# Attention of a hybrid decoder: scores and products that alternate between the two heads of a pair

## Chip, cores and metric

The kernel runs on one core of a Trainium2 chip. The metric is the device time of one execution in microseconds; a profile of one execution shows what each engine did. PE is TensorE (PEld its weight loads), DVE is VectorE, ACT is ScalarE, SP issues the DMAs.

## What is computed

Two decoder layers on 256 tokens of width 1024, everything in float32. Each layer projects the normalised tokens once and gives the columns to three mixers (a convolution, NSA attention and dilated attention), joins them with an output projection, and adds a feed-forward block with a short convolution. Cut to what bears on the change:

```python
for l in range(2):
    h = rms_norm(x, attn_norm[l])
    parts = split(h @ w_in[l])
    y_a = conv_module(...)          # 31 taps
    y_b = nsa_mixer(...)            # 8 query heads of 64, 2 key heads; compressed + selected + window
    y_c = dilated_mixer(...)        # 4 heads, 3 groups (widths 128/512/2048, strides 1/4/16)
    x = x + concat(y_a, y_b, y_c) @ w_out[l]
    x = x + conv_ffn(rms_norm(x, ffn_norm[l]), ...)

def masked_softmax(s, mask):        # in every attention
    s = where(mask, s, -1e30)
    e = where(mask, exp(s - max(s)), 0)
    return e / sum(e)
```

## The kernel before

Tokens are two tiles of 128. The dense projections split each f32 operand into a high and a low part and make three matmuls of them (L412 to L414); the weights arrive by DMA in pieces of 128 x 1024 or so, ScalarE writes the high part (L209), VectorE the low part (L212). The dense matmuls of the dilated queries, keys and values (tiles Dq, Dk, Dv) and of the output projection (oa, ob) stand around the attention work on PE.

Heads come in pairs: head j of a pair has its 64 features in partitions 64j to 64j+63 of the query and key tiles, and its output in partitions 64j to 64j+63 of the output bank. A score matmul of one head therefore reads half of the partitions (its shape is shown as 64*128), and a product matmul writes half of them (128*64). All are plain f32, and each shows as two records in the trace.

`nsa_pair(pair)`: for the first 128 queries one matmul per head (L699) fills one half of the score tile `sc` each; four masked minima (L703) read it. The scores are stored with the opposite sign, so the minimum stands for the maximum. For the second 128 queries (L710, L711) each head takes the tile in turn: its scores against 256 keys of the first kind in one bank, against 16 compressed and 256 window keys in the other, then two masked minima (L714) and one addition for the compressed keys. Then ScalarE takes exponentials and scales (L721, L725, L209), PE transposes the probabilities (L737, L743), and ScalarE copies them to `pT`. `nsa_finish(g)` multiplies them with the values: per head four matmuls (L775, L776), then one for the compressed part (L777), all into the one output bank `o`.

`dil_scores(jp)`: for the first 128 queries three matmuls per head (L847), one masked minimum each (L850); for the second, three matmuls of 256 keys per head (L857) and one masked minimum over 768 columns (L859), head by head, each followed by its exponentials (L863), transposes (L869, L876) and copies to `dpT`. `dil_pv(jp)`: six matmuls per head (L888, L890).

The score tile `sc` covers two banks of PSUM and there is one of it, so whoever writes it next waits until it has been read. Steps are written down in this order in each layer:

```python
ORDER = "np(0) dq(0) t(6) np(1) dk(0) t(6) nf(0) np(2) dv(0) t(6) np(3) nf(1) da(0) dq(1) t(10) dk(1) t(100) ds(1) dv(1) ct(0) pv(1)"
```

(np = `nsa_pair`, nf = `nsa_finish`, dq/dk/dv = dilated projections, t = convolution taps on VectorE, ds/pv = `dil_scores`/`dil_pv`, da both, ct = end of the convolution.) The framework's planner turns this into a fixed order for each engine when the program is built: it takes the earliest step whose inputs it believes ready by its own costs, and fills with later ones. So matmuls of Dq stand between the scores of np(0) in the trace. On the chip each engine works through its fixed order and waits where an input is late.

Of the kernel before, what the change touches and what calls it, by code (L numbers as in the profile page):

```python
# [12 lines left out]
F32 = mybir.dt.float32  # L13
# [3 lines left out]
ALU = mybir.AluOpType  # L17
AX = mybir.AxisListType

P = 128  # L20
D = 1024
KT = D // P
S = 256
# [164 lines left out]
def tile_hybrid_trunk(ctx, tc, x_in, pos_in, stream, feats, gains, norms, const_in, out):  # L188
# [13 lines left out]
    def sc_bank(nm):  # L202
        return ps.tile([P, 1024], F32, tag="sc", name=nm, bufs=1)
# [260 lines left out]
    for l in range(L):  # L464
# [222 lines left out]
        def nsa_pair(pair):  # L687
                g, pr = divmod(pair, 2)
                if pr == 0:
                    nsa_state[g] = (mp.tile([P, NT, 4, 16], F32, tag="cs", name=f"cs{g}", bufs=2), [])  # L690
                cs, pTs = nsa_state[g]
                negm = mp.tile([P, 2, 2, 2], F32, tag="negm", name=f"negm{pair}", bufs=2)
                dd = mp.tile([P, 2, 2, 2], F32, tag="dd", name=f"dd{pair}", bufs=2)
                ms0 = mp.tile([P, 2, 2, P], F32, tag="ms", name=f"ms0{pair}", bufs=4)
                msl = [mp.tile([P, 2, 2, P], F32, tag="ms", name=f"ms1{pair}{j}", bufs=4) for j in range(2)]
                sc = sc_bank(f"sc0{pair}")
                for j in range(2):
                    hp_ = slice(j * 64, j * 64 + 64)
                    nc.tensor.matmul(sc[:, j * 512:j * 512 + 272], QT[hp_, pair, 0:P], KG[g][hp_, P:P + 272], start=True, stop=True)  # L699
                for j in range(2):  # L700
                    for w in range(2):
                        o = j * 512 + w * 144
                        nc.vector.tensor_tensor_reduce(out=ms0[:, j, w, :], in0=sc[:, o:o + P], in1=edge[:, P:2 * P], op0=ALU.add, op1=ALU.min,  # L703
                                                       scale=1.0, scalar=3.0e38, accum_out=negm[:, 0, j, w:w + 1])
                tt(cs[:, 0, 2 * pr:2 * pr + 2, :], sc.rearrange("p (j c) -> p j c", j=2)[:, :, P:P + 16],
                   cmadd[:, 0, :].unsqueeze(1).broadcast_to([P, 2, 16]), ALU.add)
                for j in range(2):
                    hp_ = slice(j * 64, j * 64 + 64)
                    sc = sc_bank(f"sc1{pair}{j}")
                    nc.tensor.matmul(sc[:, 0:256], QT[hp_, pair, P:2 * P], KG[g][hp_, 0:256], start=True, stop=True)  # L710
                    nc.tensor.matmul(sc[:, 512:784], QT[hp_, pair, P:2 * P], KG[g][hp_, 256:528], start=True, stop=True)  # L711
                    for w in range(2):
                        o = w * 528
                        nc.vector.tensor_tensor_reduce(out=msl[j][:, w].rearrange("p a b -> p (a b)"), in0=sc[:, o:o + 256],  # L714
                                                       in1=edge[:, P - w * P:3 * P - w * P], op0=ALU.add, op1=ALU.min,
                                                       scale=1.0, scalar=3.0e38, accum_out=negm[:, 1, j, w:w + 1])
                    tt(cs[:, 1, 2 * pr + j, :], sc[:, 512:528], cmadd[:, 1, :], ALU.add)
                for j in range(2):
                    for w in range(2):
                        m = ms0[:, j, w, :]  # L720
                        nc.scalar.activation(out=m, in_=m, func=AF.Exp, scale=-1.0, bias=negm[:, 0, j, w:w + 1], accum_out=dd[:, 0, j, w:w + 1])  # L721
                for j in range(2):
                    for w in range(2):
                        m = msl[j][:, w]
                        nc.scalar.activation(out=m, in_=m, func=AF.Exp, scale=-1.0, bias=negm[:, 1, j, w:w + 1], accum_out=dd[:, 1, j, w:w + 1])  # L725
                ddf = dd.rearrange("p q j w -> p (q j w)")
                nc.vector.reciprocal(out=ddf, in_=ddf)
                gv = sg.rearrange("p t (h s) -> p t h s", s=3)[:, :, 2 * pair:2 * pair + 2, 1:3]
                tt(dd, dd, gv, ALU.mult)
                pT2 = []  # L730
                for j in range(2):
                    pT = mp.tile([P, 3, 3, P], F32, tag="pT", name=f"pT{pair}{j}", bufs=4)[:, 0:2]
                    for w in range(2):
                        copy_act(ms0[:, j, w, :], ms0[:, j, w, :], scale=dd[:, 0, j, w:w + 1])
                    tp = tp_bank(f"tp0{pair}{j}")
                    for w in range(2):
                        nc.tensor.transpose(tp[:, w * P:(w + 1) * P], ms0[:, j, w, :], ident)  # L737
                    copy_act(pT[:, :, 0, :], tp[:, 0:256].rearrange("p (a c) -> p a c", a=2))
                    for w in range(2):
                        copy_act(msl[j][:, w], msl[j][:, w], scale=dd[:, 1, j, w:w + 1])  # L740
                    tp = tp_bank(f"tp1{pair}{j}")
                    for i, (w, e) in enumerate(((0, 1), (0, 0), (1, 0), (1, 1))):
                        nc.tensor.transpose(tp[:, i * P:(i + 1) * P], msl[j][:, w, e, :], ident)  # L743
                    copy_act(pT[:, :, 1:3, :], tp.rearrange("p (a k c) -> p a k c", a=2, k=2))
                    pT2.append(pT)
                pTs.append(pT2)

        def nsa_finish(g):
# [18 lines left out]
            for pr in range(2):  # L767
                pair = 2 * g + pr
                ob = o_bank(f"o{pair}")
                for j in range(2):  # L770
                    pT = pTs[pr][j]
                    os_ = ob[j * 64:j * 64 + 64, 0:S]
                    for w in range(2):
                        vv = [vN[:, t, w, g * 64:g * 64 + 64] for t in range(NT)]
                        nc.tensor.matmul(os_, vv[0], pT[:, w, 0:2, :].rearrange("p a c -> p (a c)"), start=(w == 0), stop=False, skip_group_check=True)  # L775
                        nc.tensor.matmul(os_[:, P:S], vv[1], pT[:, w, 2, :], start=False, stop=False, skip_group_check=True)  # L776
                nc.tensor.matmul(ob[:, 0:S], vbig[:, g, 2 * pr:2 * pr + 2].rearrange("p a d -> p (a d)"), pc, start=False, stop=True, skip_group_check=True)  # L777
                copy_act(yT_hi[:, 2 + pair, :], ob[:, 0:S])
                tt(yT_lo[:, 2 + pair, :], ob[:, 0:S], yT_hi[:, 2 + pair, :].bitcast(F32), ALU.subtract)
# [56 lines left out]
        def dil_scores(jp):  # L836
# [4 lines left out]
            pTs = []  # L841
            m0s = []
            sc = sc_bank(f"dsc0{jp}")
            for j in range(2):
                hp_ = slice(j * 64, j * 64 + 64)
                for g in range(3):
                    nc.tensor.matmul(sc[:, j * 512 + g * P:j * 512 + (g + 1) * P], dq[hp_, g, 0:P], dk[hp_, g, 0:P], start=True, stop=True)  # L847
            for j in range(2):
                m0 = mp.tile([P, 3, P], F32, tag="ms", name=f"dm0{jp}{j}", bufs=4)
                nc.vector.tensor_tensor_reduce(out=m0, in0=sc[:, j * 512:j * 512 + 384].rearrange("p (g c) -> p g c", g=3), in1=dm[:, :, P:2 * P],  # L850
                                               op0=ALU.add, op1=ALU.min, scale=1.0, scalar=3.0e38, accum_out=negm[:, 0, j:j + 1])
                m0s.append(m0)
            for j in range(2):
                hp_ = slice(j * 64, j * 64 + 64)
                sc = sc_bank(f"dsc1{jp}{j}")
                for g in range(3):
                    nc.tensor.matmul(sc[:, g * 256:(g + 1) * 256], dq[hp_, g, P:S], dk[hp_, g, :], start=True, stop=True)  # L857
                m1 = mp.tile([P, 768], F32, tag="ms", name=f"dm1{jp}{j}", bufs=4)
                nc.vector.tensor_tensor_reduce(out=m1, in0=sc[:, 0:768], in1=dilm, op0=ALU.add, op1=ALU.min, scale=1.0, scalar=3.0e38,  # L859
                                               accum_out=negm[:, 1, j:j + 1])  # L860
                m0 = m0s[j].rearrange("p g c -> p (g c)")
                for q, m in ((0, m0), (1, m1)):
                    nc.scalar.activation(out=m, in_=m, func=AF.Exp, scale=-1.0, bias=negm[:, q, j:j + 1], accum_out=dd[:, q, j:j + 1])  # L863
# [17 lines left out]
        def dil_pv(jp):  # L881
            dv, pTs = dil_state["v"], dil_state["p"]
            ob = (tp_bank if jp else o_bank)(f"do{jp}")
            for j in range(2):
                os_ = ob[j * 64:j * 64 + 64, 0:S]
                for g in range(3):
                    c = (2 * g + j) * 64
                    nc.tensor.matmul(os_, dv[:, 0, c:c + 64], pTs[j][:, g, 0:2, :].rearrange("p a c -> p (a c)"), start=(g == 0), stop=False,  # L888
                                     skip_group_check=True)
                    nc.tensor.matmul(os_[:, P:S], dv[:, 1, c:c + 64], pTs[j][:, g, 2, :], start=False, stop=(g == 2), skip_group_check=True)  # L890
            copy_act(yT_hi[:, 6 + jp, :], ob[:, 0:S])
            tt(yT_lo[:, 6 + jp, :], ob[:, 0:S], yT_hi[:, 6 + jp, :].bitcast(F32), ALU.subtract)

# [142 lines left out]
```

## Time and profile before

| | |
|---|---|
| median of 3 runs | 777.91 us (777.12 to 778.69) |
| span of the profiled execution | 776.1 us; the page gives no other time of it |
| busy: PE, VectorE, ScalarE | 751.1, 598.8, 489.9 us |
| attention stretches | 74 to 190 us (layer 0), 453 to 568 us (layer 1) |

The span runs from the first to the last instruction. A matmul's end is modelled, so a group's length is best read from its start to the start of the group that follows. In the views in order of time a row gives start, length, engine, line, operation, the tiles written and read, shape and the number of records merged; rows of one line that overlap others are merged too.

### The profile page before, as it was taken

How to read it: one execution, taken by the hardware profiler on the slowest of the kernel's cores; microseconds unless marked ns; L12 is line 12 of the kernel's file. 1: busy time of each engine (PE TensorE's matmuls, PEld its weight loads, DVE VectorE, ACT ScalarE, POOL GpSimd, SP SyncE). 2: the span in 40 equal slices, each digit the busy share in tenths (PEclk: the TensorE clock that was granted, in tenths of full speed). 3: DMA queues.
4: the chain of work that ended last, by engine and by line, in shares of the span. 5: the costliest groups of instructions: out<-in, count | busy, mean ns of one | idle time of the engine just before them, and what ended most of it. 6: DMA issues, size and time to landing. Idle time of an engine off the chain costs nothing.

```text
span 776.1 us, 13412 instructions
## 1 busy us (share of the span) xinstructions
PE 751.1 (97%) x4798; PEld 657.5 (85%) x4798; DVE 598.8 (77%) x1376; ACT 489.9 (63%) x1178; POOL 22.3 (3%) x57
## 2 busy tenths in 40 slices
PE   3999999999999999999999999999999999999997
PEld 3779787887899999988868977779779999999886
DVE  5799898786898888864487798788768988888441
ACT  4766898656486667653348589876546766666330
POOL 4100000000000000000040000000000000000000
PEclk9999999999999999999999999999999999999999
DMA  8664122361465555565447231224344656665631
GB/s 290 220 208 125 60 76 88 106 208 46 162 232 198 174 197 180 190 200 191 161 149 260 83 122 42 66 98 142 130 136 146 194 188 196 179 195 187 197 124 55
DMA packets 36147, 120.29 MB, mean 155 GB/s; under 512 B 4128, under 2 KB 4400, under 8 KB 36080
## 3 DMA queue, kind: packets, MB, share of 16 engines
q1 hardware_dynamic: 35856, 119.15, 46.7%
q8 instruction: 38, 0.62, 0.3%
q0 software_dynamic: 224, 0.28, 0.2%
q14 instruction: 29, 0.24, 0.1%
HBM read 118.37 MB, written 1.05 MB: 154 GB/s over the span
## 4 chain that ended last, share of the span: by engine, by line
PE 83%; DVE 7%; ACT 5%; DMA 3%; issue 2%; SPq 0%; DVEq 0%; ACTq 0%
PE up L413 10%; PE up L412 10%; PE up L414 10%; DMA raw<-in_stream 3%; PE da L412 3%; PE da L414 3%; PE da L413 3%; PE db L412 2%; PE db L414 2%; PE db L413 2%; ACT whi L209 2%; DVE wlo L212 2%; PE dsc L857 2%; PE o L775 2%; PE Dk L412 1%
## 5 line engine op out<-in xcount | busy, mean ns | idle before, releaser
L212 DVE TENSOR_TENSOR wlo<-raw,whi 128x1024 fp32r<-128x1024 f32 (+3 forms) x232 | 259.4, 1126 | 94.6 <-ACT whi L209 93.9
L209 ACT ACTIVATE whi<-raw 128x1024 fp32r<-128x1024 f32 (+3 forms) x232 | 224.6, 979 | 116.1 <-PE db L414 54.6
L413 PE MATMUL up<-xT_lo,whi 128*128 128x256 f32 x640 | 179.2, 280 | 0.0
L412 PE MATMUL up<-xT_hi,whi 128*128 128x256 f32 x640 | 178.7, 279 | 0.0
L414 PE MATMUL up<-xT_hi,wlo 128*128 128x256 f32 x640 | 178.6, 279 | 0.0
L412 PEld LDWEIGHTS up<-xT_hi,whi 128*128 128x128 f32 x640 | 120.3, 188 | 0.0
L413 PEld LDWEIGHTS up<-xT_lo,whi 128*128 128x128 f32 x640 | 120.1, 188 | 0.0
L414 PEld LDWEIGHTS up<-xT_hi,wlo 128*128 128x128 f32 x640 | 119.7, 187 | 0.0
L222 DVE SCALAR_TENSOR_TENSOR u<-up,ffeat,u 128x255 f32<-128x255 f32 (+1 forms) x176 | 79.9, 477 | 2.6
L222 DVE SCALAR_TENSOR_TENSOR acc<-a_pad,dwh,acc 128x256 f32<-128x256 f32 x120 | 53.7, 477 | 0.4 <-ACT acc L677 0.2
L989 ACT ACTIVATE sl<-u 128x256 f32<-128x256 f32 x44 | 18.1, 416 | 47.7 <-DVE u L222 47.7
L982 ACT ACTIVATE u<-up,ffeat 128x256 f32<-128x256 f32 x88 | 44.1, 551 | 0.0
L412 PE MATMUL db<-whi,gT_hi 128*128 128x512 f32 x88 | 34.7, 394 | 0.0
L412 PE MATMUL da<-whi,gT_hi 128*128 128x512 f32 x88 | 34.7, 394 | 0.0
L414 PE MATMUL db<-whi,gT_lo 128*128 128x512 f32 x88 | 34.5, 392 | 0.0
L414 PE MATMUL da<-whi,gT_lo 128*128 128x512 f32 x88 | 34.5, 392 | 0.0
L413 PE MATMUL da<-wlo,gT_hi 128*128 128x512 f32 x88 | 34.2, 388 | 0.0
L413 PE MATMUL db<-wlo,gT_hi 128*128 128x512 f32 x88 | 34.1, 388 | 0.0
L412 PE MATMUL A<-whi,xT_hi 128*128 128x280 f32 (+1 forms) x64 | 23.7, 371 | 4.7 <-ACT xT_hi L209 4.7
L209 ACT ACTIVATE ms<-ms,dd 128x128 f32<-128x128 f32 (+1 forms) x64 | 24.6, 447 | 0.2 <-DVE dd L212 0.2
L414 PE MATMUL A<-whi,xT_lo 128*128 128x280 f32 (+1 forms) x64 | 23.5, 370 | 0.5 <-DVE xT_lo L212 0.5
L413 PE MATMUL A<-wlo,xT_hi 128*128 128x280 f32 (+1 forms) x64 | 23.3, 363 | 0.2 <-DVE wlo L212 0.2
(335 smaller groups left out, 1611.2 us busy)
## 6 DMA issues: line engine op xcount, KB each, us to landing
raw<-in_stream SPq DMA_DIRECT2D x172, 512.0 KB, 4.2
raw<-in_stream SPq DMA_DIRECT2D x48, 384.0 KB, 3.1
raw<-in_stream SPq DMA_DIRECT2D x8, 280.0 KB, 5.4
gain<-in_norms SPq DMA_DIRECT2D x4, 512.0 KB, 4.4
w<-in_stream SPq DMA_DIRECT2D x4, 512.0 KB, 6.5
x<-in_x SPq DMA_DIRECT2D x4, 256.0 KB, 5.7
out<-x SPq DMA_DIRECT2D x4, 256.0 KB, 2.0
feat<-in_feats SPq DMA_DIRECT2D x2, 339.0 KB, 4.7
```

What stands on the lines that cost most here:

```text
L209: return nc.scalar.activation(out=o, in_=i, func=AF.Copy, **kw)
L212: return nc.vector.tensor_tensor(out=o, in0=a, in1=b, op=op)
L222: return nc.vector.scalar_tensor_tensor(out=o, in0=a, scalar=s, in1=b, op0=op0, op1=op1)
L412: nc.tensor.matmul(o, a_hi, b_hi, start=start, stop=False)
L413: nc.tensor.matmul(o, a_hi, b_lo, start=False, stop=False)
L414: nc.tensor.matmul(o, a_lo, b_hi, start=False, stop=stop)
L775: nc.tensor.matmul(os_, vv[0], pT[:, w, 0:2, :].rearrange("p a c -> p (a c)"), start=(w == 0), stop=False, skip_group_check=True)
L857: nc.tensor.matmul(sc[:, g * 256:(g + 1) * 256], dq[hp_, g, P:S], dk[hp_, g, :], start=True, stop=True)
L982: nc.scalar.activation(out=u[:, h], in_=z, func=AF.Identity, scale=c[:, 2:3], bias=c[:, 3:4])
L989: nc.scalar.activation(out=sl_, in_=u[:, 0], func=AF.Silu)
```

## The change

Scores of the second query tile and products with the probabilities are issued alternately for head 0 and head 1. For NSA scores the score tile is now filled per kind of keys, one bank per head, where it was filled per head, one bank per kind of keys; the two additions for the compressed keys become one. The dilated scores of the second tile go in two rounds over both heads (groups 0 and 1, then group 2), so that each head stays in one bank; the masked minimum over 768 columns becomes one over 512 and one over 256, the second starting from the first one's result (`part`). The exponentials, transposes and copies are as before.

```diff
@@ nsa_pair, second query tile
-                for j in range(2):
-                    hp_ = slice(j * 64, j * 64 + 64)
-                    sc = sc_bank(f"sc1{pair}{j}")
-                    nc.tensor.matmul(sc[:, 0:256], QT[hp_, pair, P:2 * P], KG[g][hp_, 0:256], start=True, stop=True)
-                    nc.tensor.matmul(sc[:, 512:784], QT[hp_, pair, P:2 * P], KG[g][hp_, 256:528], start=True, stop=True)
-                    for w in range(2):
-                        o = w * 528
+                for w in range(2):
+                    sc = sc_bank(f"sc1{pair}{w}")
+                    keys = KG[g][:, 0:256] if w == 0 else KG[g][:, 256:528]
+                    n = 256 + 16 * w
+                    for j in range(2):
+                        hp_ = slice(j * 64, j * 64 + 64)
+                        nc.tensor.matmul(sc[:, j * 512:j * 512 + n], QT[hp_, pair, P:2 * P], keys[hp_], start=True, stop=True)
+                    for j in range(2):
+                        o = j * 512 + 16 * w
                         nc.vector.tensor_tensor_reduce(out=msl[j][:, w].rearrange("p a b -> p (a b)"), in0=sc[:, o:o + 256],
...
-                    tt(cs[:, 1, 2 * pr + j, :], sc[:, 512:528], cmadd[:, 1, :], ALU.add)
+                tt(cs[:, 1, 2 * pr:2 * pr + 2, :], sc.rearrange("p (j c) -> p j c", j=2)[:, :, 0:16],
+                   cmadd[:, 1, :].unsqueeze(1).broadcast_to([P, 2, 16]), ALU.add)
@@ nsa_finish
-                for j in range(2):
-                    pT = pTs[pr][j]
-                    os_ = ob[j * 64:j * 64 + 64, 0:S]
-                    for w in range(2):
-                        vv = [vN[:, t, w, g * 64:g * 64 + 64] for t in range(NT)]
-                        nc.tensor.matmul(os_, vv[0], pT[:, w, 0:2, :].rearrange("p a c -> p (a c)"), start=(w == 0), stop=False, skip_group_check=True)
-                        nc.tensor.matmul(os_[:, P:S], vv[1], pT[:, w, 2, :], start=False, stop=False, skip_group_check=True)
+                for w in range(2):
+                    vv = [vN[:, t, w, g * 64:g * 64 + 64] for t in range(NT)]
+                    for j in range(2):
+                        nc.tensor.matmul(ob[j * 64:j * 64 + 64, 0:S], vv[0], pTs[pr][j][:, w, 0:2, :].rearrange("p a c -> p (a c)"),
+                                         start=(w == 0), stop=False, skip_group_check=True)
+                    for j in range(2):
+                        nc.tensor.matmul(ob[j * 64:j * 64 + 64, P:S], vv[1], pTs[pr][j][:, w, 2, :], start=False, stop=False, skip_group_check=True)
@@ dil_scores: L847 with g outside and j inside, and
+            m1s = [mp.tile([P, 768], F32, tag="ms", name=f"dm1{jp}{j}", bufs=4) for j in range(2)]
+            part = mp.tile([P, 2], F32, tag="dpart", name=f"dpart{jp}", bufs=2)
+            for g0, g1 in ((0, 2), (2, 3)):
+                sc = sc_bank(f"dsc1{jp}{g0}")
+                for g in range(g0, g1):
+                    for j in range(2):
+                        hp_ = slice(j * 64, j * 64 + 64)
+                        nc.tensor.matmul(sc[:, j * 512 + (g - g0) * 256:j * 512 + (g - g0 + 1) * 256], dq[hp_, g, P:S], dk[hp_, g, :],
+                                         start=True, stop=True)
+                for j in range(2):
+                    nc.vector.tensor_tensor_reduce(out=m1s[j][:, g0 * 256:g1 * 256], in0=sc[:, j * 512:j * 512 + (g1 - g0) * 256],
+                                                   in1=dilm[:, g0 * 256:g1 * 256], op0=ALU.add, op1=ALU.min, scale=1.0,
+                                                   scalar=part[:, j:j + 1] if g0 else 3.0e38,
+                                                   accum_out=negm[:, 1, j:j + 1] if g0 else part[:, j:j + 1])
             for j in range(2):
-                hp_ = slice(j * 64, j * 64 + 64)
-                sc = sc_bank(f"dsc1{jp}{j}")
-                for g in range(3):
-                    nc.tensor.matmul(sc[:, g * 256:(g + 1) * 256], dq[hp_, g, P:S], dk[hp_, g, :], start=True, stop=True)
-                m1 = mp.tile([P, 768], F32, tag="ms", name=f"dm1{jp}{j}", bufs=4)
-                nc.vector.tensor_tensor_reduce(out=m1, in0=sc[:, 0:768], in1=dilm, op0=ALU.add, op1=ALU.min, scale=1.0, scalar=3.0e38,
-                                               accum_out=negm[:, 1, j:j + 1])
+                m1 = m1s[j]
@@ dil_pv
-            for j in range(2):
-                os_ = ob[j * 64:j * 64 + 64, 0:S]
-                for g in range(3):
+            for g in range(3):
+                for j in range(2):
                     c = (2 * g + j) * 64
...
+                for j in range(2):
+                    c = (2 * g + j) * 64
```

## Rows read from the trace of the kernel before

**Rows 1.** Spans: core, time from first to last instruction, mean granted TensorE clock.

```profile
core 0: 776.1 us, clock 0.999
```

**Rows 2.** Busy time by stage: stretch, length, busy us (instructions) by engine, clock, DMA.

```profile
74.00:146.00 72.00, 72.00 (x414) 55.55 (x413) 62.23 (x223) 59.48 (x204) 0.00 (x0) 1.00 0.27 85
95.00:120.00 25.00, 25.00 (x152) 20.21 (x151) 23.23 (x94) 23.22 (x87) 0.00 (x0) 1.00 0.26 81
146.00:190.00 44.00, 43.83 (x246) 37.16 (x244) 33.69 (x94) 26.59 (x85) 0.00 (x0) 1.00 0.36 117
453.00:526.00 73.00, 73.00 (x406) 54.27 (x406) 61.66 (x220) 63.58 (x226) 0.00 (x0) 1.00 0.24 79
526.00:568.00 42.00, 41.19 (x233) 34.75 (x232) 32.56 (x93) 23.80 (x64) 0.00 (x0) 1.00 0.37 115
```

**Rows 3.** PE in order of time, first scores of pair 0 (NSA).

```profile
74.57 0.73 PE L699 MATMUL sc<-KG,QT 64*128 64x272 f32 x4
75.23 0.44 PE L414 MATMUL Dq<-whi,xT_lo 128*128 128x384 f32 x1
...
77.51 0.70 PE L710 MATMUL sc<-KG,QT 64*128 64x256 f32 x2
...
78.59 0.44 PE L414 MATMUL Dq<-whi,xT_lo 128*128 128x384 f32 x1
```

**Rows 4.** PE in order of time, the first and the last split score group.

```profile
86.65 0.70 PE L710 MATMUL sc<-KG,QT 64*128 64x256 f32 x2
87.28 0.44 PE L743 MATMUL tp<-ident,ms 128*128 128x128 f32 x2
87.65 0.72 PE L711 MATMUL sc<-KG,QT 64*128 64x272 f32 x2
...
478.94 0.70 PE L710 MATMUL sc<-KG,QT 64*128 64x256 f32 x2
```

**Rows 5.** PE in order of time, products of pair 1 (NSA).

```profile
117.68 0.65 PE L775 MATMUL o<-pT,vN 128*64 128x256 f32 x2
118.16 0.38 PE L776 MATMUL o<-pT,vN 128*64 128x128 f32 x2
118.38 0.65 PE L775 MATMUL o<-pT,vN 128*64 128x256 f32 x4
...
119.08 0.59 PE L775 MATMUL o<-pT,vN 128*64 128x256 f32 x2
...
119.83 0.70 PE L777 MATMUL o<-pc,vbig 64*128 64x256 f32 x2
```

**Rows 6.** PE in order of time, dilated products of layer 0, first pair.

```profile
142.20 0.65 PE L888 MATMUL do<-dpT,dv 128*64 128x256 f32 x2
...
145.65 0.44 PE L413 MATMUL Dq<-wlo,xT_hi 128*128 128x384 f32 x1
```

**Rows 7.** PE in order of time, dilated scores of layer 0, first pair.

```profile
124.27 1.26 PE L847 MATMUL dsc<-dk,dq 64*128 64x128 f32 x12
125.47 0.45 PE L412 MATMUL Dq<-whi,xT_hi 128*128 128x384 f32 x1
...
128.30 1.13 PE L857 MATMUL dsc<-dk,dq 64*128 64x256 f32 x4
129.36 0.66 PE L743 MATMUL tp<-ident,ms 128*128 128x128 f32 x4
...
132.17 1.56 PE L857 MATMUL dsc<-dk,dq 64*128 64x256 f32 x6
133.66 0.44 PE L412 MATMUL Dq<-whi,xT_hi 128*128 128x384 f32 x1
```

**Rows 8.** VectorE groups by form: count, busy us, mean ns, idle before and releaser.

```profile
L714 DVE CUSTOM_DVE_ANT_0 ms<-sc,cst 128x256 f32<-128x256 f32 x32 | 12.5, 421 | 8.3 <-PE sc L711 6.6 <-ACT ms L209 0.9 <-ACT ms L721 0.7
L859 DVE CUSTOM_DVE_ANT_0 dm<-dsc,cst 128x768 f32<-128x768 f32 x8 | 7.6, 956 | 1.7 <-PE dsc L857 1.4
```

**Rows 9.** ScalarE in order of time, copies of head 1's dilated probabilities.

```profile
141.29 1.40 ACT L209 ACTIVATE dpT<-dtp 128x384 f32<-128x384 f32 x3
```

More of the change, by code (lines that the diff above doesn't have):

```diff
@@ L852, in dil_scores @@
                 m0s.append(m0)
-            for j in range(2):
-                hp_ = slice(j * 64, j * 64 + 64)
-                sc = sc_bank(f"dsc1{jp}{j}")
-                for g in range(3):
-                    nc.tensor.matmul(sc[:, g * 256:(g + 1) * 256], dq[hp_, g, P:S], dk[hp_, g, :], start=True, stop=True)
-                m1 = mp.tile([P, 768], F32, tag="ms", name=f"dm1{jp}{j}", bufs=4)
-                nc.vector.tensor_tensor_reduce(out=m1, in0=sc[:, 0:768], in1=dilm, op0=ALU.add, op1=ALU.min, scale=1.0, scalar=3.0e38,
-                                               accum_out=negm[:, 1, j:j + 1])
+            m1s = [mp.tile([P, 768], F32, tag="ms", name=f"dm1{jp}{j}", bufs=4) for j in range(2)]
[4 more added lines that the diff above has]
+                    for j in range(2):
+                        hp_ = slice(j * 64, j * 64 + 64)
+                        nc.tensor.matmul(sc[:, j * 512 + (g - g0) * 256:j * 512 + (g - g0 + 1) * 256], dq[hp_, g, P:S], dk[hp_, g, :],
[5 more added lines that the diff above has]
+                                                   accum_out=negm[:, 1, j:j + 1] if g0 else part[:, j:j + 1])
+            for j in range(2):
+                m1 = m1s[j]
                 m0 = m0s[j].rearrange("p g c -> p (g c)")
@@ L883, in dil_pv @@
             ob = (tp_bank if jp else o_bank)(f"do{jp}")
-            for j in range(2):
-                os_ = ob[j * 64:j * 64 + 64, 0:S]
-                for g in range(3):
+            for g in range(3):
+                for j in range(2):
                     c = (2 * g + j) * 64
-                    nc.tensor.matmul(os_, dv[:, 0, c:c + 64], pTs[j][:, g, 0:2, :].rearrange("p a c -> p (a c)"), start=(g == 0), stop=False,
+                    nc.tensor.matmul(ob[j * 64:j * 64 + 64, 0:S], dv[:, 0, c:c + 64], pTs[j][:, g, 0:2, :].rearrange("p a c -> p (a c)"),
+                                     start=(g == 0), stop=False, skip_group_check=True)
+                for j in range(2):
+                    c = (2 * g + j) * 64
+                    nc.tensor.matmul(ob[j * 64:j * 64 + 64, P:S], dv[:, 1, c:c + 64], pTs[j][:, g, 2, :], start=False, stop=(g == 2),
                                      skip_group_check=True)
-                    nc.tensor.matmul(os_[:, P:S], dv[:, 1, c:c + 64], pTs[j][:, g, 2, :], start=False, stop=(g == 2), skip_group_check=True)
             copy_act(yT_hi[:, 6 + jp, :], ob[:, 0:S])
```

## The prediction

> **What bounds the kernel now.** I read the spans first: one core, 776.1 us, TensorE granted its full clock throughout [rows 1]. The page gives no other time for the profiled execution; the three timed runs are 777.12 to 778.69 us, so about 1.8 us at the median lie outside the span, and I take those as unchanged.
>
> Next, busy time by stage [rows 2], in the two stretches of each layer where attention runs. The reader is to see three things. PE is busy for all of 74 to 146 us and of 453 to 526, and all but 1.0 us of the two later stretches: dense projection matmuls fill whatever attention leaves open. VectorE and ScalarE are not far behind: in the first stretch 62.2 and 59.5 us of 72 (86% and 83%), in layer 1 61.7 and 63.6 of 73. And within 95 to 120 us both are at 93%. So PE time taken away shortens the stretch, but not without limit.
>
> Last, PE in order of time, around the changed lines. An f32 matmul is two records here, so "x4" is two matmuls. L699 gives one matmul to each head, whose operands lie in opposite halves of the partitions; L710 and L711 give two matmuls to one head. From the first record to the next dense matmul the former takes 75.23 - 74.57 = 0.66 us, the latter 78.59 - 77.51 = 1.08 [rows 3]. The columns are nearly the same (2 x 272 against 256 + 272), so the two heads of L699 run side by side and those of L710 and L711 one behind the other. That comparison is the whole case for the change.
>
> **Part 1: NSA scores of the second query tile.** Each L710/L711 group becomes a group like L699: -0.42 us. There are 16 (2 layers, 4 pairs, 2). In 12 the two matmuls stand together; in 4 the planned order puts transposes between them, as between 86.65 and 87.65 us, the last at 478.94 [rows 4]. Split so, heads can't overlap and the pieces cost 0.63 and 0.65 us, as now. I assume the same four: 12 x 0.42 = 5.0 us; all sixteen joined would give 6.7 and a little more.
>
> **Part 2: NSA products.** The present order issues all of head 0, then all of head 1, yet the rows show overlap: 117.68 to 118.38 is head 0 alone (0.70 us), 118.38 to 119.08 holds four records a line, two of each head, and 119.08 to 119.83 is head 1 alone (0.75) [rows 5]. Full alternation turns the two lone stretches into one shared one: 2.15 becomes 0.70 + 0.70 + 0.10 for the offset and the change to the next shape, 1.50; -0.65 each. Of 8 groups 6 stand in one piece: 6 x 0.65 = 3.9 us (8 would give 5.2). The Trainium skill (TensorE: Matmul & The Clock Gate, Part 3, "The mechanism") says that matmuls start and end strictly in program order. By that rule today's group would have no shared stretch and take 2.85 us, the change would save 1.35 on each of 8 and the sum below would be some 5.6 us larger for these products; this trace disagrees, since records of head 1 share 118.38 to 119.08 with those of head 0 that stand ahead of them in the program, and the rows decide.
>
> **Part 3: dilated products.** One group takes 142.20 to 145.65 = 3.45 us [rows 6]. It has six matmuls a head against four, so by the same stretches an alternating group is 3 x 0.70 + 0.05 = 2.15: -1.30. Of 4 groups, 3 stand whole: 3.9 us (4 give 5.2).
>
> **Part 4: dilated scores.** First tile (L847): 124.27 to 125.47 = 1.20 us for 12 records, six per head, which already share some time. Alternating: 1.20 - 0.34 = 0.86, the 0.34 being three of them at the 0.11 us that a 128-column record takes in rows 5 (118.38 - 118.16 for two); 4 x 0.34 = 1.4 us. Second tile (L857): one head is six records, 132.17 to 133.66 = 1.49 us, so two heads 2.98. After, a first round has four records per head and a second has two. Four records of one head took 129.36 - 128.30 = 1.06 [rows 7], two of the same width 0.63 [rows 4], and the other head runs beside them: 1.69, so -1.29; 4 x 1.29 = 5.2. Two of the eight heads stand split now, the first at 128.30; I take 3/4 in the early stretches and all in the late ones, 3.9.
>
> **Part 5: VectorE's edits.** The masked minimum over 768 columns (956 ns) becomes one over 512 and one over 256. The 256 takes 421 ns; 512 lies between the two, by their slope (535 ns for 512 columns) near 690. [rows 8]. That adds about 0.16 us, and one more read of an accumulator, eight times: under 2 us of the 190 in these stages. Sixteen small additions for the compressed keys become eight of twice the width; I count nothing for that. The 2 us lie beside PE's dense matmuls; with that cover gone they would cost at most their own size. The head-0 dilated chain starts later, since its second score round has to wait for both heads' first reads of the single score buffer; head 1's starts earlier. ScalarE and the transposes queue behind that. With dense matmuls ahead in PE's order nobody stands still; without them it would be the two reductions, 0.69 + 0.42 us, four times: 4.5 us, a bound that I keep for the upper end. No DMA moves.
>
> **The sum.** PE's own time: 5.0 + 3.9 + 3.9 + 1.4 + 3.9 = 18.1 us, between 0 if everything is split and 23.7 (6.7 + 5.2 + 5.2 + 1.4 + 5.2) if nothing is. Of it the late stretches hold two of four dilated steps, all whole now: 2 x (0.34 + 1.29 + 1.30) = 5.9; the early ones 12.2.
>
> What arrives at the end: the late stretches have room (VectorE 33.7 of 44 us, 32.6 of 42), 5.9 counts whole. In the early ones I let the busier engine rise to the 93% of 95 to 120 us and no further, as the highest share seen with PE never waiting: layer 0 can shrink to 62.23 / 0.93 = 66.9, by 5.1 us; layer 1 to 63.58 / 0.93 = 68.4, by 4.6. That is 9.7, under the 12.2. So 9.7 + 5.9 = 15.6 us: a span near 760.5, and 777.9 - 15.6 = **762.3 us**.
>
> **Rivals.**
> *The whole sum arrives.* ScalarE and VectorE wait for PE in some places now (VectorE stood idle 6.6 us for L711's scores before L714 [rows 8]), so they speed up with it, and their weight conversions can slide to the later stretch. Time: 777.9 - 18.1 to 23.7 = 754 to 760. Against it: 93% already.
>
> *ScalarE or VectorE becomes the bound at once.* Each score still has to be masked, exponentiated, scaled and copied, none of which shrinks. If the present 86% is all that an engine with chained waits can reach, the early stretches give nothing and only 5.9 us remain, less up to 4.5 for the later head-0 chain: 772.0 to 776.5. PE would then show waits at the transposes (L737, L743). The Trainium skill (TensorEngine Tiling, "PSUM Bottleneck") warns of this: array tiling speeds up the matmuls but not the emptying of PSUM, which can become the bottleneck. No row of before shows it happening; the 93% stretch shows it is near.
>
> *No change in the overlap:* the planner puts transposes between the heads nearly everywhere. Then products keep the overlap they have and each score pair costs 1.28 as in rows 4; nothing is gained, 777 to 779. The 12 of 16 groups that stand whole speak against it.
>
> *Slower: in-order PE waits for head 1's probabilities.* Today head 0's products cover the copies of head 1. Alternating, the second matmul already needs head 1, and all dense matmuls queue behind it on PE. The copies of both remaining blocks and the first one run on ScalarE from 141.29 to 142.69 [rows 9], and the first product starts at 142.20: a wait of 0.5 us at most there. There are 12 product groups, so the change turns slower where the mean wait exceeds 18.1 / 12 = 1.5 us. At 2 us it would be 777.9 - 18.1 + 24 = 784. The planner places an instruction where it believes its inputs ready, so a mean of 1.5 us is unlikely.
>
> **Chances.** Forecast, 758 to 767 us: 0.50. Whole sum, 754 to 760: 0.17. Helpers bound, 767 to 776.5: 0.22. No change: 0.04. Slower: 0.07. Faster by over 0.2%, which is about what a measurement of this kernel tells from none (1.6 us): 0.50 + 0.17 + 0.22 = 0.89; within: 0.04; slower: 0.07. The range runs from the lower end of the whole sum to most of the helpers' case, 754 to 774; the forecast's own is 758 to 767.
>
> **What the profile after would show.** The second-tile score groups at about 0.66 us, with four records under one line; products of NSA at about 1.50 and dilated at 2.15 us, with all records shared; PE records of the same number. Stages 74 to 146 and 453 to 526 shorter by about 5 us each with ScalarE or VectorE at 93% or more, the later ones by about 3 each. I am wrong if score groups still take 1.08 (split or not side by side), if PE shows waits for ScalarE of over 3 us in a layer's early stretch, or if a product group contains a stall.

## The result

| | before | after |
|---|---|---|
| median | 777.99 us (777.12 to 778.69, 4 runs) | 759.25 us (758.76 to 759.89, 4 runs) |
| span of the profiled execution | 776.1 us [rows 1] | 757.3 us |

The ratio is 0.9767, with a 95% interval of 0.9755 to 0.9779: 18.7 us faster by the medians, 18.8 by the spans. The forecast was 762.3 us (758 to 767).

Span and granted clock after, to be held against [rows 1]:

```profile
core 0: 757.3 us, clock 0.999
```

Busy time by stage after, in the columns of [rows 2]. The first three lines lie in layer 0, the last two in layer 1:

```profile
73.50:143.00 69.50, 69.50 (x435) 52.07 (x434) 65.02 (x234) 62.68 (x230) 0.00 (x0) 1.00 0.30 95
93.00:118.00 25.00, 25.00 (x162) 19.37 (x161) 24.16 (x96) 24.55 (x94) 0.00 (x0) 1.00 0.26 81
143.00:183.00 40.00, 39.69 (x237) 33.20 (x236) 33.61 (x91) 26.09 (x64) 0.00 (x0) 1.00 0.45 147
444.00:514.00 70.00, 69.96 (x431) 52.47 (x430) 64.23 (x233) 64.12 (x231) 0.00 (x0) 1.00 0.28 91
514.00:552.00 38.00, 37.01 (x221) 30.68 (x220) 32.03 (x88) 24.79 (x62) 0.00 (x0) 1.00 0.42 140
```

The clock is the same, so the time came from the work. PE is still busy for every microsecond of the first stretch (69.50 of 69.50) and all but 0.04 us of layer 1's. Beside it VectorE now stands at 65.02 of 69.50 (94%), and between 93 and 118 us ScalarE at 24.55 of 25 (98%), where [rows 2] had both at 93%.

PE in order of time after: score groups, products and dilated groups, with the record that follows each, which gives its length:

```profile
77.01 0.70 PE L713 MATMUL sc<-KG,QT 64*128 64x256 f32 x4
77.64 0.44 PE L414 MATMUL Dq<-whi,xT_lo 128*128 128x384 f32 x1
...
85.29 0.70 PE L713 MATMUL sc<-KG,QT 64*128 64x256 f32 x2
85.91 0.44 PE L746 MATMUL tp<-ident,ms 128*128 128x128 f32 x2
86.28 0.70 PE L713 MATMUL sc<-KG,QT 64*128 64x256 f32 x2
86.91 0.44 PE L740 MATMUL tp<-ident,ms 128*128 128x128 f32 x2
...
113.93 0.48 PE L713 MATMUL sc<-KG,QT 64*128 64x256 f32 x1
113.94 0.48 PE L780 MATMUL o<-pc,vbig 64*128 64x256 f32 x1
...
115.73 0.65 PE L776 MATMUL o<-pT,vN 128*64 128x256 f32 x4
116.21 0.39 PE L779 MATMUL o<-pT,vN 128*64 128x128 f32 x4
...
117.18 0.70 PE L780 MATMUL o<-pc,vbig 64*128 64x256 f32 x2
...
121.06 0.94 PE L850 MATMUL dsc<-dk,dq 64*128 64x128 f32 x12
121.93 0.58 PE L740 MATMUL tp<-ident,ms 128*128 128x128 f32 x2
...
124.68 0.70 PE L863 MATMUL dsc<-dk,dq 64*128 64x256 f32 x4
125.31 0.78 PE L746 MATMUL tp<-ident,ms 128*128 128x128 f32 x4
...
138.54 0.65 PE L898 MATMUL do<-dpT,dv 128*64 128x256 f32 x2
139.12 0.44 PE L887 MATMUL dtp<-ident,dm 128*128 128x128 f32 x2
...
139.84 0.43 PE L898 MATMUL do<-dpT,dv 128*64 128x256 f32 x1
...
141.94 0.44 PE L412 MATMUL Dk<-whi,xT_hi 128*128 128x384 f32 x1
...
167.71 1.13 PE L863 MATMUL dsc<-dk,dq 64*128 64x256 f32 x8
168.78 0.50 PE L413 MATMUL oa<-wlo,yT_hi 128*128 128x512 f32 x1
...
179.80 0.65 PE L898 MATMUL do<-dpT,dv 128*64 128x256 f32 x4
...
181.90 0.51 PE L414 MATMUL ob<-whi,yT_lo 128*128 128x512 f32 x1
```

How each group answers to one of before:

- A whole score group of the second tile takes 77.64 - 77.01 = 0.63 us, where [rows 3] had 1.08. Nine of the 16 stand like that. Seven are split, as between 85.29 and 86.91: 0.62 and 0.63 us, the price of both pieces in [rows 4]. Two of the seven found another partner: head 1 of the group that began at 112.94 runs beside the compressed product L780, which uses the other half of the partitions and starts 0.01 us later (113.93 and 113.94); in layer 1 (482.57) the same two meet for one record each.
- NSA products take 117.18 - 115.73 = 1.45 us, against 2.15 in [rows 5].
- Dilated products take 181.90 - 179.80 = 2.10 us, against 3.45 in [rows 6]. Each layer's first pair has its first matmul split off (138.54; two records are one matmul).
- Dilated scores of the first tile take 121.93 - 121.06 = 0.87 us, against 1.20 in [rows 7]. Those of the second, standing whole, have a first round of 168.78 - 167.71 = 1.07 us; the early ones come in pieces of 0.63 (124.68).

Summing, by tile and line, the time from each PE record's start to the next one's, from the first score to the first transpose after the output projection (in us):

| | layer 0 before | after | layer 1 before | after |
|---|---|---|---|---|
| NSA scores, first tile | 2.64 | 2.64 | 3.27 | 2.64 |
| NSA scores, second tile | 8.77 | 6.44 | 9.26 | 7.39 |
| NSA products, compressed too | 11.13 | 8.29 | 11.65 | 8.39 |
| dilated scores, first tile | 2.39 | 1.73 | 2.39 | 1.74 |
| dilated scores, second tile | 6.15 | 3.59 | 6.35 | 4.21 |
| dilated products | 6.90 | 4.78 | 7.04 | 4.77 |
| all other matmuls | 90.41 | 91.71 | 88.50 | 89.56 |
| whole stretch | 128.39 | 119.18 | 128.46 | 118.70 |

The attention groups give 21.3 us. Of these, 0.6 are first-tile NSA scores whose code did not change: layer 1 had one such group split before and has none after. In layer 1 a score and a compressed product start together at 482.89, so 0.3 us could stand in either of their two rows. The other matmuls take 2.4 us back, among them the dense matmuls and the transposes. The obvious reading, more changes of shape, does not come out of the traces: neighbouring PE records in the two stretches differ in the rows and columns of the array that they use about equally often, 127 times before and 126 after. Why these matmuls became dearer stays open. The net is 19.0 us, where the spans differ by 18.8: what lies outside these stretches is unchanged but for 0.2 us.

By place: from the first score to the first matmul that ends the convolution, layer 0 goes from 74.57 to 165.12 us before (90.55) to 74.07 to 158.38 after (84.31), and layer 1 from 90.08 to 83.03. The early part gives 6.2 and 7.1 us, the rest of the two stretches 3.0 and 2.7.

VectorE's groups after, in the columns of [rows 8]:

```profile
L716 DVE CUSTOM_DVE_ANT_0 ms<-sc,cst 128x256 f32<-128x256 f32 x32 | 12.5, 421 | 4.0 <-PE sc L713 2.0 <-ACT pT L209 0.8 <-PE tp L746 0.8
L866 DVE CUSTOM_DVE_ANT_0 dm<-dsc,cst 128x512 f32<-128x512 f32 x8 | 5.3, 675 | 0.0
L866 DVE CUSTOM_DVE_ANT_0 dm<-dsc,cst,dpart 128x256 f32<-128x256 f32 x8 | 3.5, 481 | 0.1
```

The masked minima kept their price (421 ns), but VectorE stands idle before them for 4.0 us where it was 8.3, and only 2.0 of that is for PE's scores (6.6 before). The split dilated minimum costs 675 + 481 - 956 = 200 ns more, eight times, 1.6 us in all.

For the scores the change altered the order and also which bank each head writes. Banks alone do not explain the overlap: L710 and L711 wrote two different banks too and took 1.08 us, while the products overlap inside the one output bank.

### The profile page after: what moved, and what is told of

Read it like the earlier page. It is cut to its first block, busy times and chain, and to the rows that moved or that the text cites. A ratio compares the mean times of both kernels' runs of the same rounds, so it can differ in the third digit from the quotient of the medians.

```text
span 757.3 us, 13407 instructions
## 1 busy us (share of the span) xinstructions
PE 731.0 (97%) x4798; PEld 638.8 (84%) x4798; DVE 598.4 (79%) x1384; ACT 487.1 (64%) x1178; POOL 22.3 (3%) x57
## 3 DMA queue, kind: packets, MB, share of 16 engines
HBM read 118.37 MB, written 1.05 MB: 158 GB/s over the span
## 4 chain that ended last, share of the span: by engine, by line
PE 82%; DVE 8%; ACT 5%; DMA 3%; issue 2%; SPq 0%; DVEq 0%; ACTq 0%
PE up L413 10%; PE up L414 10%; PE up L412 10%; DMA raw<-in_stream 3%; PE da L412 3%; PE da L413 3%; PE da L414 3%; PE db L412 3%; PE db L413 2%; PE db L414 2%; DVE wlo L212 2%; ACT whi L209 2%; PE sc L713 2%; PE Dk L412 2%; PE Dk L413 2%
## 5 line engine op out<-in xcount | busy, mean ns | idle before, releaser
L1002 ACT ACTIVATE sl<-u 128x256 f32<-128x256 f32 x44 | 18.1, 416 | 47.7 <-DVE u L222 47.7
```

Of the source, the lines that this page charges most:

```text
L1002: nc.scalar.activation(out=sl_, in_=u[:, 0], func=AF.Silu)
```

## Experiments: the four parts one at a time

Each kernel is the one before with one part of the change. The question is whether each part is worth its own term, and whether the parts add up.

**Scores of the second NSA tile alone.**

```diff
-                for j in range(2):
-                    sc = sc_bank(f"sc1{pair}{j}")
...
+                for w in range(2):
+                    sc = sc_bank(f"sc1{pair}{w}")
...
+                    for j in range(2):
+                        hp_ = slice(j * 64, j * 64 + 64)
+                        nc.tensor.matmul(sc[:, j * 512:j * 512 + n], QT[hp_, pair, P:2 * P], keys[hp_], start=True, stop=True)
```

> Only the NSA scores of the second query tile alternate. Theory (each part saves PE's own time in its groups, and PE is the bound): the sixteen groups go from 18.1 to about 14.1 us of PE time as in the profile after, and the whole kernel gets 3.5 to 5 us faster (ratio 0.9935 to 0.9955). Rival (the gain comes from another order of the surrounding work, or needs all parts): within 1.5 us of before.

Measured: 773.18 us beside 777.64, ratio 0.9941 (0.9929 to 0.9954), -4.5 us. Its trace has the second-tile scores at 6.45 and 7.39 us a layer, the same as in the whole change.

**NSA products alone.**

```diff
-                for j in range(2):
...
-                    for w in range(2):
...
+                for w in range(2):
...
+                    for j in range(2):
+                        nc.tensor.matmul(ob[j * 64:j * 64 + 64, 0:S], vv[0], pTs[pr][j][:, w, 0:2, :].rearrange("p a c -> p (a c)"),
...
+                    for j in range(2):
+                        nc.tensor.matmul(ob[j * 64:j * 64 + 64, P:S], vv[1], pTs[pr][j][:, w, 2, :], start=False, stop=False, skip_group_check=True)
```

> Only the NSA products alternate. Theory: each of eight groups goes from 2.15 to 1.45 us, so 5 to 6.5 us faster (ratio 0.9915 to 0.9935). Rival (the heads already overlap enough, or another engine takes the time back): under 2 us.

Measured: 772.96 us, 0.9941 (0.9929 to 0.9953), -4.7 us, a little under the 5 to 6.5 expected. One group in each layer is still split; these products fall by 5.1 us in the trace.

**Dilated scores alone.**

```diff
-                for g in range(3):
-                    nc.tensor.matmul(sc[:, g * 256:(g + 1) * 256], dq[hp_, g, P:S], dk[hp_, g, :], start=True, stop=True)
+            for g0, g1 in ((0, 2), (2, 3)):
+                for g in range(g0, g1):
+                    for j in range(2):
+                        nc.tensor.matmul(sc[:, j * 512 + (g - g0) * 256:j * 512 + (g - g0 + 1) * 256], dq[hp_, g, P:S], dk[hp_, g, :],
```

> Only the dilated scores alternate, with the two reductions for one. Theory: four first-tile groups 1.19 to 0.87 us, four second-tile steps 2.98 to 1.70, so 5 to 6 us faster (ratio 0.992 to 0.9935). Rival (the later start of head 0's chain and the extra reductions cost what PE saves): within 1.5 us of before.

Measured: 773.87 us, 0.9955 (0.9942 to 0.9967), -3.8 us, less than expected. In its trace, summed as in the table, the dilated scores of both tiles fall by 5.4 us (layer 1's second tile from 6.35 only to 4.82, because its rounds are split); other matmuls take 0.5 of that back and the products 0.1. The two stretches together are 4.7 us shorter (128.39 to 125.59 and 128.46 to 126.58). The spans differ by 4.1 (776.1 to 772.0). Where the rest goes is open; it is inside the interval's half width of about 1 us.

**Dilated products alone.**

```diff
-            for j in range(2):
-                for g in range(3):
+            for g in range(3):
+                for j in range(2):
...
+                for j in range(2):
```

> Only the dilated products alternate. Theory: four groups 3.45 to 2.10 us or a little more, so 4 to 5.4 us faster (ratio 0.993 to 0.995). Rival (PE waits for head 1's copies): a stall inside the groups of layer 0 at about 140 us and a gain under 2 us. If the four parts add up to the 18.7 us of the whole change, no engine but PE holds back any of it.

Measured: 772.74 us, 0.9936 (0.9923 to 0.995), -4.9 us. Layer 0's first group goes from 141.49 to 143.76, 2.27 us in one piece.

Together 4.5 + 4.7 + 3.8 + 4.9 = 17.9 us, against 18.7 for the whole change: the parts add up within their intervals. Had the helper engines cut the early gain, as the forecast had it, the parts together would have brought less than one by one.

## Experiment: must the heads alternate matmul by matmul?

The kernel after, with each head's two matmuls of a kind kept together: two of head 0, then two of head 1, and so on.

```diff
                                          start=(w == 0), stop=False, skip_group_check=True)
-                    for j in range(2):
                         nc.tensor.matmul(ob[j * 64:j * 64 + 64, P:S], vv[1], pTs[pr][j][:, w, 2, :], start=False, stop=False, skip_group_check=True)
...
-                for j in range(2):
-                    c = (2 * g + j) * 64
                     nc.tensor.matmul(ob[j * 64:j * 64 + 64, P:S], dv[:, 1, c:c + 64], pTs[j][:, g, 2, :], start=False, stop=(g == 2),
```

> The whole change, but products in blocks of two matmuls: head 0 both, head 1 both, then the next kind of keys. Theory (TensorE starts records of the other head's column half while up to four records of the first still stand ahead in the program): the blocks overlap as fully as single alternation, groups at 1.45 to 1.55 and 2.10 to 2.25 us, time within 1 us of the change as it stands (ratio to before 0.976 to 0.978). Rival (only neighbours overlap, records start in program order): NSA groups near 2.1 us, dilated ones near 3.2, and 8 to 9 us of the gain lost (ratio near 0.988).

Measured: 759.67 us beside 777.36, ratio 0.9769 (0.9755 to 0.9782), the same as the change. Its PE in order of time, an NSA and a dilated group:

```profile
116.28 0.66 PE L776 MATMUL o<-pT,vN 128*64 128x256 f32 x4
116.77 0.40 PE L778 MATMUL o<-pT,vN 128*64 128x128 f32 x4
...
117.78 0.70 PE L779 MATMUL o<-pc,vbig 64*128 64x256 f32 x2
...
180.48 0.66 PE L897 MATMUL do<-dpT,dv 128*64 128x256 f32 x4
...
182.63 0.50 PE L414 MATMUL ob<-whi,yT_lo 128*128 128x512 f32 x1
```

The groups take 117.78 - 116.28 = 1.50 and 182.63 - 180.48 = 2.15 us, 0.05 more than when alternating. Head 1's first record starts although both matmuls of head 0 (L776, L778) stand ahead of it in the program: the "x4" of 116.28 are two L776 records of each head, and L778 starts only at 116.77. So records of the other half of the array run ahead of program order, as the forecast had read out of [rows 5], and PE departs here from the fixed order in which an engine works. They do so only so far. In the kernel before, with four matmuls of head 0 ahead of head 1's, 0.70 us at each end stayed alone. With six, as in [rows 6], head 1 joined after four of them, 143.55 - 142.20 = 1.35 us:

```profile
143.55 0.65 PE L888 MATMUL do<-dpT,dv 128*64 128x256 f32 x4
```

In both, the last two matmuls of head 0 (four records) were still to start or just starting. The rule of the Trainium skill that the forecast had weighed (TensorE: Matmul & The Clock Gate, Part 3, "The mechanism"), strict program order in start and end, does not hold for the starts in these groups; ends are modelled in these profiles and can't show it.

## Experiments: are VectorE or ScalarE the bound now?

The forecast had them cap the early stretches. If they do, less work for them must shorten the kernel.

**Half of the convolution's taps, after and before.** VectorE's taps 16 to 30 are left out (the convolution then covers 16 taps of 31; the expectations count VectorE's 15 alone), about 14 us of VectorE's work a layer.

```diff
-        taps = [(b, k) for k in range(1, TAPS) for b in range(2)]
+        taps = [(b, k) for k in range(1, 16) for b in range(2)]
```

In the kernel after:

> The whole change with half of the convolution taps left out (30 instead of 60 per layer, 14 us of VectorE work per layer; the convolution is computed with 15 taps). If VectorE holds the changed kernel back in the early stretches (busy 65 of 69.5 us there), relief should give 2 us or more beyond what the same relief gives the kernel before. If PE alone is the bound: within 1 us of the change as it stands.

In the kernel before, as the control:

> The kernel before with the same half of the convolution taps left out (the convolution is computed with 15 taps), as the control: PE is never idle in its early stretches, so within 1 us of before by both theories.

Measured: after, 758.79 us beside 777.36, ratio 0.9765 (0.9752 to 0.9779): no gain over the change's 0.9767. Before, 779.3 us, ratio 1.0024 (1.0015 to 1.0033): 1.9 us slower with less work, where at most 1 us either way was expected. PE's work stands in another order when the taps are gone; from first score to the transposes, layer 0 then takes 130.81 us in place of 128.39 and layer 1 127.48 in place of 128.46. So moves of up to 2 us, most likely from the planner's order, must be reckoned with, and the null result after the change needed a second test, on a kernel whose score groups are kept whole.

**Score groups kept whole.** The kernel after, with the score matmuls ranked ahead of other steps by the planner, so that nothing is put between the heads:

```diff
+                    with tc.high_priority():
                         for j in range(2):
                             hp_ = slice(j * 64, j * 64 + 64)
                             nc.tensor.matmul(sc[:, j * 512:j * 512 + n], QT[hp_, pair, P:2 * P], keys[hp_], start=True, stop=True)
```

(and the same around the first-tile NSA scores and the dilated scores of the second tile).

> The whole change, and every score group keeps its matmuls together: the planner ranks score matmuls ahead of all else as soon as their inputs are ready. Theory (a split group loses the overlap, and seven of sixteen NSA groups and two of the eight dilated rounds are split after the change): each group made whole saves 0.6 us of PE time, 5 us in all, so 754 to 756 us (ratio to before 0.969 to 0.972). Rival (the transposes that now come later delay ScalarE's copies and PE waits for them): no faster than the change, 759 us or more.

Its control is the kernel before with the same ranking of its own, unalternated score matmuls:

> The kernel before, with the same ranking of its score matmuls ahead of all else (no alternation). It is the control for the version with whole pairs. Theory (that version gains because a whole group holds both heads side by side): here a whole group holds one head, so only the four split groups and one split first-tile group are mended, at some 0.2 us of shape changes each: 0 to 2 us faster, 775.5 to 777.5 (ratio 0.997 to 1.0). Rival (earlier scores help by themselves): 4 us or more faster.

Measured: with the change 754.33 us (753.48 to 755.02), ratio 0.9703 (0.969 to 0.9716), 4.9 us under the change. The control 776.77, ratio 0.9984 (0.9975 to 0.9992): 1.05 us. PE in order of time with ranking, in the place where the change had its first split groups:

```profile
85.37 0.70 PE L715 MATMUL sc<-KG,QT 64*128 64x256 f32 x4
86.00 0.66 PE L748 MATMUL tp<-ident,ms 128*128 128x128 f32 x4
...
87.83 0.73 PE L715 MATMUL sc<-KG,QT 64*128 64x272 f32 x4
88.49 0.44 PE L748 MATMUL tp<-ident,ms 128*128 128x128 f32 x2
```

0.63 and 0.66 us a group. All 16 stand whole: 5.17 and 5.15 us a layer where the change has 6.44 and 7.39, and the second-tile dilated scores 3.30 and 3.30 in place of 3.59 and 4.21. That is 4.7 us of PE's time; products, now split more, take 1.1 back, other matmuls give 0.6, and the two stretches come out 4.3 us shorter. So most of this is heads that run side by side, which the control does not have, and not scores that come earlier.

Its windows over the early stretches:

```profile
73.50:142.50 69.00, 68.62 (x438) 51.91 (x437) 65.72 (x230) 60.62 (x216) 0.00 (x0) 1.00 0.30 91
442.00:510.00 68.00, 67.22 (x433) 50.75 (x432) 64.85 (x228) 63.91 (x228) 0.00 (x0) 1.00 0.31 94
```

VectorE is at 95% in both, ScalarE at 94% in the second, and PE still has all but 0.4 and 0.8 us. Each helper was now relieved on top of this version.

**Half of the taps left out with whole groups** (same edit of the taps):

> The version with whole pairs, and half of the convolution taps left out (30 instead of 60 per layer; the convolution is computed with 15 taps). VectorE is busy 65.7 of 69.0 us in its early stretch. If VectorE has become the bound there: 2 us or more faster than whole pairs alone (under 752.3). If PE still is: within 1.5 us of 754.3.

**ScalarE's scaling left out with whole groups** (the probabilities miss their normalisation and gate; eight activations fewer per pair):

```diff
-                    for w in range(2):
-                        copy_act(ms0[:, j, w, :], ms0[:, j, w, :], scale=dd[:, 0, j, w:w + 1])
...
-                    for w in range(2):
-                        copy_act(msl[j][:, w], msl[j][:, w], scale=dd[:, 1, j, w:w + 1])
```

> The version with whole pairs, and ScalarE's eight scalings of the NSA probabilities per pair left out (the probabilities stay without their normalisation and gate): 14 us less of ScalarE work per layer and a shorter chain from scores to transposes. If ScalarE or that chain has become the bound in the early stretches: 4 us or more faster than whole pairs alone (under 750.3). If PE is: within 2 us of 754.3.

Measured: 754.65 us, ratio 0.9704 (0.9691 to 0.9716), without half the taps; 755.77 us, 0.9716 (0.9704 to 0.9729), without the scaling. Neither is faster than 754.33. Windows of the first:

```profile
73.50:142.00 68.50, 68.09 (x433) 51.24 (x432) 55.46 (x202) 60.45 (x214) 0.00 (x0) 1.00 0.29 89
```

and of the second:

```profile
73.50:142.00 68.50, 68.50 (x436) 52.15 (x435) 65.14 (x231) 50.60 (x183) 0.00 (x0) 1.00 0.28 83
442.00:510.00 68.00, 67.34 (x427) 50.08 (x427) 63.62 (x226) 52.00 (x186) 0.00 (x0) 1.00 0.30 91
```

The relief arrived (VectorE 65.72 to 55.46 us, ScalarE 60.62 to 50.60 and 63.91 to 52.00), and PE is as busy as before it. An engine that works 95% of a stretch beside a full PE did not set its length. The other page of the Trainium skill that stood in the forecast (TensorEngine Tiling, "PSUM Bottleneck") says that emptying PSUM may take over as the limit after a fourfold speedup; here at most two heads run side by side. No run here bears it out: taking work off either of the two engines that read PSUM gave nothing, though the work taken off did not itself read PSUM. Both were not relieved at once; with PE idle for at most 0.8 of 68 us there was little for that to gain.

## Why the prediction was right, and where it failed

**Direction and mechanism: right.** The comparison in [rows 3] was the whole case, and it carries over: groups in alternation cost 0.63 to 0.66 us, and the parts alone bring 17.9 of the 18.7 us.

**The step that failed: the cap on the early stretches.** "I let the busier engine rise to the 93% of 95 to 120 us and no further", which cut 12.2 us to 9.7. The early part gave 6.2 + 7.1 = 13.3 us, uncapped. 93% was only the highest share that the kernel before had shown; it was never shown to be a limit. After the change it is 94% over the whole stretch and 98% in its densest 25 us, and the relief runs show no bound at 95%. What the rival "the whole sum arrives" said is what happened: the helpers had waited for PE's scores (6.6 us of L714's idle time in [rows 8], 2.0 after), and sped up with it. 759.25 lies in both its range and the forecast's, so that it fell within 758 to 767 is luck as far as the cap goes: the range reached down into the rival's.

**Part 1: shares.** The price held (0.42 saved forecast; 1.08 to 0.63 or 0.66 measured), the count did not: 7 of 16 groups stood split and not 4. 4.2 us by the trace, 4.5 alone, against 5.0. The ranked version shows what the three more and the four cost.

**Part 2: undersized, the largest miss of the five parts.** All eight groups stand in one piece after, seven at 1.45 us and one at 1.54; at 2.15 - 1.45 = 0.70 each that is 5.6 us, where six at 0.65 were counted, 3.9. The two groups that stood split before gain a little more, and with the compressed products the trace has 6.1 us. The single-part run, where one group in each layer is still split, gave 4.7. The 5.6 us that this part names for the rule of strict order compare eight groups with eight; against the six in the sum it is 8 x 1.35 - 3.9 = 6.9.

**Part 3:** 2.10 us a group as worked out (2.15), first pairs split once; 4.4 us by the trace and 4.9 alone against 3.9.

**Part 4:** first tile 1.3 us against 1.4; second tile 1.07 + 0.63 = 1.70 whole against 1.69, and 4.7 us in all against 3.9. That 3.9 is a slip: 3/4 of the two early steps and all of the two late ones are 3.5 x 1.29 = 4.5. The sum would have been 18.7 and its early share 12.8 in place of 12.2; the cap cuts either to 9.7, so the forecast stays. The single-part run gave 3.8 of the 6.0.

**Part 5:** 0.20 us more of VectorE's time each against 0.16, and no gain when VectorE was relieved: nothing, as counted.

**The slower rival** (an in-order PE waits for head 1's probabilities) did not show. PE's waits after list nothing between 73 and 143 us. At the place named in [rows 9], ScalarE's copies of the dilated probabilities after, in order of time:

```profile
138.24 0.48 ACT L209 ACTIVATE dpT<-dtp 128x384 f32<-128x384 f32 x1
...
138.81 0.61 ACT L209 ACTIVATE dpT<-dtp 128x512 f32<-128x512 f32 x1
...
139.59 0.38 ACT L209 ACTIVATE dpT<-dtp 128x256 f32<-128x256 f32 x1
```

The last copy ends at 139.97, and the products start at 138.54; but between their first matmul and the rest (139.84) the planner put the two transposes whose copy was missing and two dense matmuls of Dk. The wait became a split: the first matmul stands alone for 139.12 - 138.54 = 0.58 us, and PE fills the time to 139.84 with other work.

**Uncounted: 2.4 us back.** The sum had no term for the other matmuls, which became dearer for a reason that stays open. Without them the sum of 18.1 would have been too low by 3.2 us; with them it came out low by 0.9.

## What to carry to other kernels

Matmuls that use one half of the array should stand next to one whose operands or outputs lie in the other half; two of the same half in a row do little harm (0.05 us a group), but a full-width matmul or transpose between the halves costs the whole gain (0.62 + 0.63 us in place of 0.63). Where a planner orders the work, look for groups that it has split and rank them: here that was worth 4.9 us, a quarter of the change itself. A helper engine at 95% beside a full PE was no bound here: relieve it by itself before counting on it as a cap.

## What was not expected of the hardware

- Matmuls of different steps pair up: head 1's score at 113.93 and the compressed product at 113.94 us, on opposite halves of the partitions, start 0.01 us apart and take 0.64 us together (to 114.57).
- In blocks of two matmuls per head the overlap is as good as in full alternation, but for 0.05 us a group (1.50 against 1.45, 2.15 against 2.10).
- Less work for a helper made the kernel before 1.9 us slower (779.3 against 777.36 us); the trace shows another order of PE's work there, which makes this more likely the planner's doing than the chip's.
